# Attention values one step earlier, beside the next scores, in an encoder kernel

## The chip, the cores and the metric

The kernel runs on one core of a Trainium2 chip. The metric is the device time of one launch in microseconds. A core has a matrix engine (TensorE, PE in the profile, with its weight loads as PEld), a vector engine (VectorE, DVE), a scalar engine (ScalarE, ACT), GpSimd (POOL) and SyncE (SP), which here issues the transfers. Each engine works through its own queue in order, and semaphores make one wait for another.

## The reference, cut to what matters

The program is a trunk of two layers over 512 tokens of width 1024, in float32. Each layer normalizes x, makes one wide projection of it, computes two kinds of attention from parts of that projection, gates and mixes them, and ends with a gated feed-forward part (SwiGLU).

```python
z = h @ w_in
# a: differential attention, 4 heads, each with two softmaxes
s = einsum('bqhcd,bkhcd->bhcqk', qblk, kk) * scale
p = softmax(s, axis=-1)
a = p[:, :, 0] - lam_full * p[:, :, 1]
o = einsum('bhqk,bkhe->bqhe', a, v)          # then rms_norm of o
# b: three groups of window attention with dilation 1, 4 and 16, 8 heads each
s = where(mask, einsum('brnqhd,brnkhd->brnhqk', qb, kn) * scale, NEG_INF)
e = exp(s - max(s)); den = sum(e)
o = einsum('brnhqk,brnkhd->brnqhd', e, vn) / den
# the three groups are combined per head by a softmax over their log denominators
m = (sigmoid(g_A) * (a @ W_a) + sigmoid(g_B) * (b @ W_b)) @ W_out
```

## The kernel before

Float32 products are made from two halves. `split_part` cuts each weight tile into a rounded `whi` (a cast on ACT, L106 or L109) and a rest `wlo` (DVE, L107 or L110); the activations stand as `hTh` and `hTl`. `mm3` (lines 121 to 123) then issues three matmuls for each pair of tiles into a PSUM tile `pj`, of which there are three. All weights come through one stream of 1 MB transfers issued on SP (`load_raw`, L88), with two split weights held ready.

PE runs in the order in which the kernel's code issues its instructions (`manual_schedule`). The other engines' orders are laid out by a planner when the program is built: it goes by the order of issue as priority, by its own estimate of when each operand is ready, and lifts the weight splits ahead.

A layer projects in pieces. For each of two head pairs of the differential attention (`da_proj`) and for each of two times three window groups (`g_proj`) it makes q, k and v. A q or k piece is `ws_gen`: four steps of 12 matmuls of 512 columns ("wide"). A v piece (`proj_v`) is four steps of 24 matmuls of 256 columns ("narrow"). After q and k comes the rotary part `rope` on DVE (L415, L419) and GpSimd (L420, L421), which frees `pj`, and another split (L458, L459).

Attention is put between these steps. `drive` runs a projection and calls `att_step` after each of its steps; `att_step` advances the first job in `attq` by one step, and a job whose last scores are a period behind it lets the next one step as well. A job is a generator made by `pipeline`: each tile or batch i passes through stages, and stage f of tile i runs at step `period * i + lag`, with a period of 4. Stages that fall on the same step run in the order in which the tuple lists them.

- Differential attention (`da_attn`, four query tiles per head pair): `scores` (matmuls L484 with 32-row operands into the PSUM tiles `at0` to `at3`, the maxima L490, exponentials L492, and the difference of both softmaxes, L496 to L500), `turn` (PE transposes L510, copies L512), `values` (matmuls L519 into `at4`, then squares L525, a mean and a power on GpSimd L75, and L529, L530), and `finish` (transposes L537 into the other half of the same `at4`, and a split L540, L541).
- Window groups (`g_attn`; group 0 has two batches, groups 1 and 2 have one): `scores` (L583, then the mask L591, the maximum L593, exponentials L596), `turn` (transposes L610 and copies L611, or for group 2 a transpose on DVE, L606), and `values` (L628 for group 0, L631 for the others, in one or two parts, then copies L635 or L638).
- `combine` weighs the three groups of a head pair. It runs alone, once all jobs before it are done: small work on DVE and ACT, three steps later three PE transposes with multiplies (L687, L689) one step apart, then the sum and its split (L691 to L695).

`turn` has lag 3, `finish` 7, `scores` 0. The lags of `values` are in the lines that change. After the second head pair the gates are projected (`gate`, L736), and what is left of the queue is run out.

Of the kernel before, what the change touches and what calls it, by code (L numbers as in the profile page):

```python
# [23 lines left out]
NT = S // P  # L24
# [9 lines left out]
def encoder_trunk_kernel(  # L34
# [23 lines left out]
    def at(i, shape=(P, S)):  # L58
        return ps.tile(list(shape), F32, tag=f"at{i}", name=nm("at"), bufs=1)
# [4 lines left out]
    def small(n):  # L64
        return pp.tile([P, n], F32, tag=f"sm{n}", name=nm("sm"), bufs=8)
# [5 lines left out]
    def rstd_of(ss, n, scale, eps):  # L71
        t = small(n)
        nc.vector.tensor_scalar(out=t, in0=ss, scalar1=scale, scalar2=eps, op0=ALU.mult, op1=ALU.add)  # L73
        r = small(n)
        nc.gpsimd.tensor_tensor(out=r, in0=t, in1=mhalf[:, 0:n], op=ALU.pow)  # L75
        return r
# [310 lines left out]
    for l in range(depth):  # L387
# [17 lines left out]
        def et(shape=(P, S), dt=F32):  # L405
            return ip.tile(list(shape), dt, tag="e", name=nm("e"), bufs=8)
# [55 lines left out]
        def qk_scores(parts, qs, ks):  # L462
            n = len(parts)
            for j, (q, k) in enumerate(parts):
                for half in range(2):
                    for c in range(4):
                        r = slice(32 * c, 32 * c + 32)
                        yield c, q[r, half, qs], k[r, half, ks], j + half == 0, j + half == n
# [9 lines left out]
        def da_attn(u, qk, v):  # L478
            st = [dict() for _ in range(NT)]

            def scores(n):
                o = [at(c) for c in range(4)]
                for c, q, k, first, last in qk_scores(qk, slice(n * P, (n + 1) * P), slice(0, S)):
                    nc.tensor.matmul(o[c], q, k, start=first, stop=last)  # L484
                st[n].update(a=[], r=[])
                for h in range(2):
                    nmx, den, es = small(2), small(2), []
                    for c in range(2):
                        oc = o[2 * h + c]
                        nc.vector.tensor_reduce(out=nmx[:, c:c + 1], in_=oc, axis=AX.X, op=ALU.max, negate=True)  # L490
                        e = et()
                        nc.scalar.activation(out=e, in_=oc, func=AF.Exp, bias=nmx[:, c:c + 1],  # L492
                                             accum_out=den[:, c:c + 1])
                        es.append(e)
                    r = small(2)
                    nc.vector.reciprocal(out=r, in_=den)  # L496
                    nl = small(1)
                    nc.vector.scalar_tensor_tensor(out=nl, in0=den[:, 0:1], scalar=neglam, in1=r[:, 1:2],
                                                   op0=ALU.mult, op1=ALU.mult)
                    nc.vector.scalar_tensor_tensor(out=es[0], in0=es[1], scalar=nl, in1=es[0],  # L500
                                                   op0=ALU.mult, op1=ALU.add)
                    st[n]["a"].append(es[0])
                    st[n]["r"].append(r)

            def turn(n):
                st[n]["aT"] = []
                for h in range(2):
                    tp = at(h, (P, 4, P))
                    for kt in range(4):
                        nc.tensor.transpose(tp[:, kt, :], st[n]["a"][h][:, kt * P:(kt + 1) * P], ident)  # L510
                    aT = et((P, 4, P))
                    nc.scalar.copy(out=aT, in_=tp)  # L512
                    st[n]["aT"].append(aT)

            def values(n):
                oo = st[n]["o"] = at(4, (P, 4, P))
                for h in range(2):
                    for kt in range(4):
                        nc.tensor.matmul(oo[:, h, :], st[n]["aT"][h][:, kt, :], v[:, kt, h * P:(h + 1) * P],  # L519
                                         start=(kt == 0), stop=(kt == 3))  # L520
                on = et((P, 2, P))
                ss = small(2)
                rr = st[n]["r"]
                for g in range(2):
                    nc.scalar.activation(out=on[:, g, :], in_=oo[:, g, :], func=AF.Square, scale=rr[g][:, 0:1],  # L525
                                         accum_out=ss[:, g:g + 1])
                rs = rstd_of(ss, 2, 1.0 / P, SUBLN_EPS)
                for g in range(2):
                    nc.vector.tensor_tensor(out=rs[:, g:g + 1], in0=rs[:, g:g + 1], in1=rr[g][:, 0:1], op=ALU.mult)  # L529
                    nc.vector.scalar_tensor_tensor(out=on[:, g, :], in0=oo[:, g, :], scalar=rs[:, g:g + 1], in1=sg,  # L530
                                                   op0=ALU.mult, op1=ALU.mult)
                st[n]["on"] = on

            def finish(n):
                tp = st[n]["o"][:, 2:4, :]
                for g in range(2):
                    nc.tensor.transpose(tp[:, g, :], st[n]["on"][:, g, :], ident)  # L537
                qs = slice(n * P, (n + 1) * P)
                hv = oaT[0][:, 2 * u:2 * u + 2, qs]
                nc.scalar.copy(out=hv, in_=tp)  # L540
                nc.vector.tensor_tensor(out=oaT[1][:, 2 * u:2 * u + 2, qs], in0=tp, in1=hv.bitcast(F32),  # L541
                                        op=ALU.subtract)

            yield from pipeline(NT, 4, ((turn, 3), (finish, 7), (values, 5), (scores, 0)))

        def pipeline(n, period, stages):
            for j in range((n - 1) * period + max(lag for _, lag in stages) + 1):
                for f, lag in stages:
                    i, r = divmod(j - lag, period)
                    if r == 0 and 0 <= i < n:  # L550
                        f(i)
                yield j >= n * period
# [18 lines left out]
        def g_attn(gi, qk, v, vs, res):  # L571
            og, sts = g_out(gi)
            nb = 2 if gi == 0 else 4
# [40 lines left out]
            def values(b, part):  # L614
                o = at(4, (P, 2, 256))
                for i in range(2 * part, 2 * part + 2):
                    n = b * nb + i
                    cols = slice((n % 2) * P, (n % 2 + 1) * P)
                    for pr in range(2):
                        for kt in range(2 if gi == 0 else 1):  # L620
                            for hh in range(2):
                                h = 2 * pr + hh
                                hs = slice(h * DH, (h + 1) * DH)
                                pt = st[b]["pt"][h]
                                if gi == 0:
                                    s = WIN_START[n] + kt * P
                                    vt = v[:, s // P, hs] if s % P == 0 else vs[:, s // P, hs]
                                    nc.tensor.matmul(o[hh * DH:(hh + 1) * DH, pr, cols], vt, pt[:, 2 * i + kt, :],  # L628
                                                     start=(kt == 0), stop=(kt == 1))
                                else:  # L630
                                    nc.tensor.matmul(o[hh * DH:(hh + 1) * DH, pr, cols], v[:, n, hs], pt[:, i, :],  # L631
                                                     start=True, stop=True)
                if gi == 0:
                    for pr in range(2):
                        nc.scalar.copy(out=og[:, pr, :].rearrange("p (r s t) -> p t s r", r=4, s=4)[:, 16 * b:16 * b + 16],  # L635
                                       in_=o[:, pr, :].rearrange("p (t s r) -> p t s r", s=4, r=4))
                else:
                    nc.scalar.copy(out=og[:, :, 256 * part:256 * part + 256], in_=o)  # L638

            parts = [((lambda b, part=part: values(b, part)), 5 + part) for part in range(nb // 2)]  # L640
            yield from pipeline(NT // nb, 4, (*parts, (turn, 3), (scores, 0)))
            res.append((og, to_class(sts) if gi == 0 else sts))

# [79 lines left out]
        for u in range(2):  # L723
            res = []
            for gi in range(3):
                att_push(g_attn(gi, *drive(g_proj(gi)), res), DELAY[1 + gi])
            att_push(combine(u, res), 0, True)
# [153 lines left out]
```

## Time and profile before

| what | value |
|---|---|
| median of 3 runs | 1857.94 us (1857.57 to 1859.06) |
| profiled execution | 1857.75 us, of which the span from first to last instruction is 1856.0 us |
| mean granted TensorE clock | 0.996 |
| PE busy | 1819.6 us, 98% of the span |
| DVE, ACT, POOL busy | 917.7, 668.2, 159.1 us |
| longest waits of PE in all | 12.5 us for the first normalized tiles (L244 for L238), 5.9 and 2.4 us for the split of h (L122 for L247, L121 for L246) |

A line of the groups or the timeline names the source line, the engine, the operation, the tile written and the tiles read, the active rows and columns of a matmul, the shape and the count. PE's durations overlap, since matmuls are pipelined: what a matmul costs is read from one start to the next. In the timeline the number in brackets is the idle time before the row and what ended it. Layer one takes the first half of the span, layer two the second, with the same waits.

### The profile page before, as it was taken

Reading aid. Unit: us, or ns where it says so; the run is one execution under the profiler, and the core shown is the slowest. Engines: PE = TensorE matmul, PEld = TensorE weight load, DVE = VectorE, ACT = ScalarE, POOL = GpSimd, SP = SyncE. Lnnn points to the kernel's source line nnn. Section 1 sums busy time; section 2 is a strip of 40 time slices with the busy share of each in tenths; the row PEclk is TensorE's granted clock in tenths of the full one; section 3 lists DMA queues with packets and bytes.
Section 4 is the critical chain, followed back from the end, with each engine's and each line's share of the span. In section 5 each row is a group of like instructions: output and inputs, shape, how many; then the busy total and the mean of one; then the engine's idle time right before and its main releaser. Section 6 shows DMA issues by size and latency. Waiting matters only on the chain. (4 is left out here: it accounts for less than half of the span.)

```text
span 1856.0 us, 25587 instructions
## 1 busy us (share of the span) xinstructions
PE 1819.6 (98%) x10784; PEld 1542.3 (83%) x10784; DVE 917.7 (49%) x1255; ACT 668.2 (36%) x1301; POOL 159.1 (9%) x128
## 2 busy tenths in 40 slices
PE   6999999999999999999999999999999999999997
PEld 6888897888889888888888888888888788888886
DVE  5667758545355333322456776675445543333222
ACT  3444453353234223222234444443523332322221
POOL 1212011101000000000011121111011000000000
PEclk9999999999999999999999999999999999999999
DMA  6322123222444322232432322322234423322332
GB/s 186 104 68 87 60 75 102 67 86 91 133 138 151 112 91 91 94 110 91 147 118 78 96 65 69 111 63 87 71 108 148 149 94 105 99 91 91 107 109 68
DMA packets 145186, 186.26 MB, mean 100 GB/s; under 512 B 7216, under 2 KB 130480, under 8 KB 145072
## 3 DMA queue, kind: packets, MB, share of 16 engines
q1 hardware_dynamic: 145072, 184.63, 31.2%
q8 instruction: 84, 1.38, 0.3%
q14 instruction: 30, 0.25, 0.0%
HBM read 174.06 MB, written 10.55 MB: 99 GB/s over the span
## 5 line engine op out<-in xcount | busy, mean ns | idle before, releaser
L121 PE MATMUL pj<-hTh,whi 128*128 128x512 f32 (+1 forms) x1536 | 588.9, 383 | 2.4 <-ACT hTh L246 2.4
L122 PE MATMUL pj<-hTl,whi 128*128 128x512 f32 (+1 forms) x1536 | 581.2, 378 | 5.9 <-DVE hTl L247 5.9
L123 PE MATMUL pj<-hTh,wlo 128*128 128x512 f32 (+1 forms) x1536 | 580.0, 378 | 0.0
L107 DVE TENSOR_TENSOR wlo<-raw,whi 128x1024 fp32r<-128x1024 f32 x252 | 331.4, 1315 | 456.2 <-ACT whi L106 455.9
L106 ACT CAST whi<-raw 128x1024 fp32r<-128x1024 f32 x252 | 264.6, 1050 | 733.6 <-PE pj L122 490.8
L121 PEld LDWEIGHTS pj<-hTh,whi 128*128 128x128 f32 x1536 | 291.4, 190 | 63.2 <-issue 6.8
L122 PEld LDWEIGHTS pj<-hTl,whi 128*128 128x128 f32 x1536 | 291.5, 190 | 56.8 <-DVE hTl L247 7.4
L123 PEld LDWEIGHTS pj<-hTh,wlo 128*128 128x128 f32 x1536 | 291.3, 190 | 53.5
L121 PE MATMUL pj<-whi,hTh 128*128 128x256 f32 x512 | 147.5, 288 | 0.0
L122 PE MATMUL pj<-wlo,hTh 128*128 128x256 f32 x512 | 144.8, 283 | 0.0
L123 PE MATMUL pj<-whi,hTl 128*128 128x256 f32 x512 | 144.8, 283 | 0.0
L75 POOL TENSOR_TENSOR sm<-sm,mhalf 128x1 f32<-128x1 f32 (+1 forms) x48 | 33.2, 692 | 921.8 <-DVE sm L73 921.8
L596 ACT ACTIVATE e<-e,gst 128x128 f32<-128x128 f32 (+1 forms) x192 | 81.4, 426 | 81.6 <-DVE gst L593 81.4
L121 PEld LDWEIGHTS pj<-whi,hTh 128*128 128x128 f32 x512 | 98.0, 191 | 3.2 <-issue 2.8
L122 PEld LDWEIGHTS pj<-wlo,hTh 128*128 128x128 f32 x512 | 98.1, 192 | 0.2
L123 PEld LDWEIGHTS pj<-whi,hTl 128*128 128x128 f32 x512 | 98.0, 191 | 0.0
L806 DVE TENSOR_TENSOR s<-s,pj 128x512 f32<-128x512 f32 x42 | 28.9, 688 | 123.6 <-PE pj L123 123.6
L285 PE MATMUL at<-whi,ac 128*128 128x512 f32 x200 | 78.8, 394 | 0.0
L284 PE MATMUL at<-whi,ac 128*128 128x512 f32 x200 | 78.5, 392 | 0.0
L286 PE MATMUL at<-wlo,ac 128*128 128x512 f32 x200 | 77.7, 388 | 0.0
L492 ACT ACTIVATE e<-at,sm 128x512 f32<-128x512 f32 x64 | 43.8, 686 | 76.4 <-DVE sm L490 76.4
L591 DVE TENSOR_TENSOR e<-at,mk 128x512 f32<-128x512 f32 x64 | 41.2, 682 | 40.1 <-PE at L583 40.1
(175 smaller groups left out, 2347.4 us busy)
## 6 DMA issues: line engine op xcount, KB each, us to landing
raw<-in_w_in_dram SPq DMA_DIRECT2D x64, 1024.0 KB, 5.7
raw<-in_w_gate_up_dram SPq DMA_DIRECT2D x44, 1024.0 KB, 5.0
raw<-in_w_down_dram SPq DMA_DIRECT2D x22, 1024.0 KB, 4.9
raw<-in_w_out_dram SPq DMA_DIRECT2D x8, 1024.0 KB, 4.9
xs<-m SPq DMA_DIRECT2D x12, 512.0 KB, 2.9
m<-xs SPq DMA_DIRECT2D x12, 512.0 KB, 4.9
m<-in_x_dram SPq DMA_DIRECT2D x32, 128.0 KB, 5.2
raw<-in_w_a_dram SPq DMA_DIRECT2D x8, 512.0 KB, 3.4
```

Of the source, the lines that this page charges most:

```text
L75: nc.gpsimd.tensor_tensor(out=r, in0=t, in1=mhalf[:, 0:n], op=ALU.pow)
L106: nc.scalar.copy(out=shp(hi), in_=src)
L107: nc.vector.tensor_tensor(out=shp(lo), in0=src, in1=shp(hi.bitcast(F32)), op=ALU.subtract)
L121: nc.tensor.matmul(o, ah, bh, start=(i == 0), stop=False)
L122: nc.tensor.matmul(o, ah, bl, start=False, stop=False)
L123: nc.tensor.matmul(o, al, bh, start=False, stop=(i == n - 1))
L284: nc.tensor.matmul(o, ah, hi[:, sl], start=(k == 0), stop=False)
L285: nc.tensor.matmul(o, al, hi[:, sl], start=False, stop=False)
L286: nc.tensor.matmul(o, ah, lo[:, sl], start=False, stop=(k == nk - 1))
L492: nc.scalar.activation(out=e, in_=oc, func=AF.Exp, bias=nmx[:, c:c + 1], accum_out=den[:, c:c + 1])
L591: nc.vector.tensor_tensor(out=e, in0=o[h], in1=mask, op=ALU.add)
L596: nc.scalar.activation(out=e[:, i, :], in_=e[:, i, :], func=AF.Exp, bias=sts[:, n, h:h + 1], accum_out=sts[:, n, 4 + h:5 + h])
```

## The change

The lag of `values` goes from 5 to 4 in both kinds of attention (from 5 and 6 to 4 and 5 where there are two parts). With a period of 4 the values of a tile or batch then fall on the step of the next one's scores, and stand ahead of them, since the tuple lists `values` before `scores`. No instruction is added or taken away.

```diff
             def da_attn(u, qk, v):
...
-            yield from pipeline(NT, 4, ((turn, 3), (finish, 7), (values, 5), (scores, 0)))
+            yield from pipeline(NT, 4, ((turn, 3), (finish, 7), (values, 4), (scores, 0)))
...
             def g_attn(gi, qk, v, vs, res):
...
-            parts = [((lambda b, part=part: values(b, part)), 5 + part) for part in range(nb // 2)]
+            parts = [((lambda b, part=part: values(b, part)), 4 + part) for part in range(nb // 2)]
             yield from pipeline(NT // nb, 4, (*parts, (turn, 3), (scores, 0)))
```

## The prediction

> **What bounds the kernel now.** I read the page first (share of each engine), then the waits of TensorE (PE), then PE's timeline around the attention steps, then that of VectorE (DVE) where PE waited.
>
> ```profile
> span 1856.0 us, 25587 instructions
> PE 1819.6 (98%) x10784; PEld 1542.3 (83%) x10784; DVE 917.7 (49%) x1255; ACT 668.2 (36%) x1301; POOL 159.1 (9%) x128
> ```
>
> PE is busy for 98% of the span, and its order is written by hand, so a change of order can win or lose two things only: what PE loses where it passes from one kind of matmul to another, and where it stands still for another engine. The first is seen in the starts of PE's instructions (start, duration, engine, line); two rows of the groups by line, with the mean in ns behind the comma, give durations used below.
>
> ```profile
> 65.11 0.39 PE L123 MATMUL pj<-hTh,wlo 128*128 128x512 f32 x1
> 65.43 1.67 PE L484 MATMUL at<-op,op 32*128 32x512 f32 x24
> 67.02 0.50 PE L121 MATMUL pj<-hTh,whi 128*128 128x512 f32 x1
> 67.36 0.39 PE L122 MATMUL pj<-hTl,whi 128*128 128x512 f32 x1
> 67.59 0.39 PE L123 MATMUL pj<-hTh,wlo 128*128 128x512 f32 x1
> ...
> 83.82 0.39 PE L123 MATMUL pj<-hTh,wlo 128*128 128x512 f32 x1
> 84.05 1.95 PE L519 MATMUL at<-m,e 128*128 128x128 f32 x16
> 85.75 0.36 PE L121 MATMUL pj<-whi,hTh 128*128 128x256 f32 x1
> 85.95 0.28 PE L122 MATMUL pj<-wlo,hTh 128*128 128x256 f32 x1
> 86.07 0.29 PE L123 MATMUL pj<-whi,hTl 128*128 128x256 f32 x1
> ```
>
> A wide projection matmul starts 0.23 us after the one before it (67.36 to 67.59), so a step of 12 is 2.72 us; a narrow one starts after 0.12, so a step of 24 is 2.88 us. Scores of the differential attention (L484, 32-row operands) cost two surcharges: they start 0.32 after the last projection (0.09 more than 0.23), and the second projection behind them comes 0.34 after the first (0.11 more). The values (L519, 128x128 operands) start at the usual 0.23; the row's 1.95 less the 0.275 that one lasts, over 15, is 0.11 a matmul, so 16 are 1.79, and the block with the longer first gap behind it is 1.70 + 0.08. An interruption by these values costs nothing.
>
> ```profile
> L519 PE MATMUL at<-m,e 128*128 128x128 f32 x256 | 31.1, 275 | 0.0
> ...
> L530 DVE SCALAR_TENSOR_TENSOR e<-at,sm,sg 128x128 f32<-128x128 f32 x32 | 9.8, 347 | 0.0
> ```
>
> ```profile
> 249.03 1.09 PE L631 MATMUL at<-e,m 128*64 128x128 f32 x16
> 250.05 2.07 PE L583 MATMUL at<-op,op 32*128 32x128 f32 x64
> 252.05 0.50 PE L121 MATMUL pj<-hTh,whi 128*128 128x512 f32 x1
> ```
>
> This is the one place where a window group's values (128x64 operands) and the next scores stand together already, at the second half of group 1.
>
> **The change, part by part.** Counting the steps of the queue with lag 5 and with lag 4 gives, for each of the two layers, 55 places where attention stands between projections before, and 45 after. Eleven blocks of values move in front of the scores that followed one step behind: eight of the differential attention (the last tile of each head pair joins the next job's first scores), three of group 0. One joint place is lost: group 1's second half now comes a step before group 2's first scores. Groups 1 and 2 and the combine that waits for them run one step earlier. No instruction is added or removed.
>
> *Passages.* Differential values cost nothing where they stood, so joining them to scores wins nothing if values-to-scores costs the 0.09 of projection-to-scores. No row shows that pair. If it is hidden like projection-to-values, 8 x 0.09 = 0.7 us a layer is won; if it is as dear as L631-to-L583 (16 matmuls take 1.02, so 0.2 from the last start, about 0.15 over its pace), 8 x 0.06 = 0.5 is lost. I take 0, since both full-height matmuls shown above hand over to each other freely. [...] A joint of group values and scores saves one 0.09 and one 0.11: 0.2, with two more joints a layer: **-0.4**.
>
> *The turns behind the joined scores.* Scores go through reduce, exponential and L500 before the transposes of `turn`, three steps later. Until now the values' 1.70 + 0.08 us lay in between. That cover is gone.
>
> ```profile
> 74.41 1.74 DVE L500 SCALAR_TENSOR_TENSOR e<-e,sm,e 128x512 f32<-128x512 f32 x1
> ...
> 88.56 1.75 DVE L500 SCALAR_TENSOR_TENSOR e<-e,sm,e 128x512 f32<-128x512 f32 x1
> ...
> 152.50 1.75 DVE L500 SCALAR_TENSOR_TENSOR e<-e,sm,e 128x512 f32<-128x512 f32 x1
> ...
> 183.86 1.27 DVE L500 SCALAR_TENSOR_TENSOR e<-e,sm,e 128x512 f32<-128x512 f32 x1
> ```
>
> ```profile
> 76.29 0.63 PE L510 MATMUL at<-ident,e 128*128 128x128 f32 x4 [0.39 <-DVE e L500]
> ...
> 91.59 0.82 PE L510 MATMUL at<-ident,e 128*128 128x128 f32 x6
> ...
> 154.86 1.04 PE L510 MATMUL at<-ident,e 128*128 128x128 f32 x8
> ...
> 186.47 1.03 PE L510 MATMUL at<-ident,e 128*128 128x128 f32 x8
> 187.65 0.44 PE L537 MATMUL at<-ident,e 128*128 128x128 f32 x2
> ```
>
> The very first turn has no values before it and waits already: L500 ends at 76.15, and PE goes on at 76.29, 0.14 later. The second head's four transposes come 0.44 after the turn starts. So the first of the seven later tiles has 91.59 + 0.44 - 90.31 = 1.72 us to spare, the worst 154.86 + 0.44 - 154.25 = 1.05, the last 186.47 + 0.44 - 185.13 = 1.78. In the same two views two others have 1.31 and 1.38, and the last two, on narrow steps, over 2.7. Less 1.78, plus 0.14, these are late by 0.20, 0.87, 0.14, 0.61 and 0.54: **+2.4** a layer. If the small norm instructions of the values, now ahead of the scores, leave DVE's chain, it could be 1.2; if they push into it (about 0.7 each, two L530 of 0.35), 5.
>
> What waits behind: next to the late turn stands `finish`. The last turn above was held up by it (186.47 to 187.65 is 1.18, not 0.88), since the normed values came late; they now have a step and the scores more time: **-0.3**. The values of tile n+1 follow one step after `finish` of tile n, whose tile `at4` they overwrite; ACT and DVE must have read it. I take 0, and up to 0.6 in one place a layer. Values that stand where scores stood need the same copies that those scores waited for (L512, L611): 0. SP's small transfers of group 0's statistics are issued one step earlier, ahead of a weight load; two weights are held ready, so 0. POOL's power step of the norm moves ahead of the ropes on its queue; POOL is busy 9% of the span, so 0.
>
> *Values one step earlier with no scores beside them.* For group 2 the turn is a DVE transpose. PE rows, then DVE rows:
>
> ```profile
> 266.22 0.55 PE L631 MATMUL at<-e,m 128*64 128x128 f32 x6
> ...
> 395.67 0.44 PE L631 MATMUL at<-e,m 128*64 128x128 f32 x4
> ```
>
> ```profile
> 263.71 0.69 DVE L606 STREAM_TRANSPOSE e<-e 128x512 f32<-128x512 f32 x1
> ...
> 392.87 0.71 DVE L606 STREAM_TRANSPOSE e<-e 128x512 f32<-128x512 f32 x1
> ```
>
> The fourth transpose ends at 264.40, and the fifth matmul of the moved values would need it at 266.22 - 2.88 + 0.25 = 263.59; in the second pair of heads 393.58 against 395.67 - 2.72 + 0.25 = 393.20. With the 0.14: 0.95 + 0.52 = **+1.5** (0.5 to 2).
>
> *The combine one step earlier.* Here DVE is behind, and PE pays:
>
> ```profile
> 296.96 1.71 PE L583 MATMUL at<-op,op 32*128 32x256 f32 x48
> ...
> 306.90 2.16 PE L610 MATMUL at<-ident,e 128*128 128x128 f32 x12
> 309.31 0.93 PE L610 MATMUL at<-ident,e 128*128 128x128 f32 x4 [0.26 <-ACT e L596]
> ...
> 312.94 0.38 PE L583 MATMUL at<-op,op 32*128 32x256 f32 x1
> ...
> 314.83 1.69 PE L583 MATMUL at<-op,op 32*128 32x256 f32 x45 [0.22 <-DVE e L611]
> ```
>
> ```profile
> 285.75 1.07 DVE L415 TENSOR_TENSOR r<-pj,cos 128x512 f32<-128x512 f32 x1 [2.44 <-PE pj L123]
> ...
> 302.64 1.28 DVE L591 TENSOR_TENSOR e<-at,mk 128x512 f32<-128x512 f32 x2
> ```
>
> 16 transposes at 0.11 last 1.8; these end at 310.24, 3.34 after their start: 1.5 lost. The scores lose 1.9 between 312.94 and 314.83. The cause is that the masks (L591) of the second head pair's group 0 start at 302.64 though their scores (296.96) were done some 4 us before: the combine's multiplies and split stand ahead of them in DVE's queue. One step earlier, the combine's first multiplies fall into the 2.44 us in which DVE was idle. Masks 2.4 to 3.2 us earlier free the turn wholly, and of the 1.9 leave about 0.5: **-2.9** (0 to -3.4).
>
> Sum a layer: 0 - 0.4 + 2.4 - 0.3 + 1.5 - 2.9 = +0.3; two layers +0.6. The profiled execution took 1857.75 us (span 1856.0 and 1.75 around it), 0.2 under the median of 1857.94. So **1858.3**.
>
> **The rivals.** *A, the forecast: gains and losses cancel*, 0.2% or 3.7 us being about what a measurement of this kernel can tell from no change. For it: every term is of 0.3 to 3 us, and they have both signs.
>
> *B, slower: the late turns.* The joined scores leave DVE too little time, and the combine's relief does not come, because DVE merely fills the gap with the same queue in another order. With turns at 2.4, the group values at 1.5, passages and `finish` at -0.7 and relief at -0.5, a layer is +2.7, the kernel 1863.2. It decides once a layer's terms together pass +1.9, which with the full group values needs relief under 1.3. Against it: DVE has idle time right where the combine moves.
>
> *C, faster: the relief without the late turns.* If the values' norm leaves the chain of the scores, the turns cost 1.2, the group values 1.0 and relief is -3.4: -1.9 a layer with the rest, 1853.9.
>
> *D, the clock.* Differential values and scores together are 1.70 + 1.59 = 3.3 us without a projection. If the granted clock fell over such a stretch, 22 following steps of 2.7 us at half pace would cost some 60 us: 1917. Against it, the stretch that exists:
>
> ```profile
> 249.03:252.05 3.02, 3.02 (x82) 2.73 (x81) 0.00 (x0) 0.58 (x1) 0.00 (x0) 1.00 0.96 299
> ```
>
> PE is busy in all of it and its clock is 1.00 (third column from the right). One in a hundred is left for the 0.3 us by which the new blocks are longer. [...]
>
> **How the numbers follow.** A 0.60, B 0.22, C 0.17, D 0.01. The time is A's, 1858.3, with its own range 1854.2 to 1861.6 (within 3.7 of the median). Of B and C I keep the nearer part: 1853.5 reaches just past C's sum, 1863.8 just past B's; turns at 5 a layer with the full relief (1863.5) lie inside, and so does each end of the passages and of the values put alone to the forecast's sum. Chances: faster 0.17, same 0.60, slower 0.23.
>
> **What the profile after would show.** Right: L519 directly before L484, with a start of L484 about 0.2 after the last L519; PE waits on L510 for L500 in several turns of a layer, 0.1 to 0.9 us each, where one is seen now; values of group 2 waiting for L606; L591 of the second pair's group 0 some 3 us earlier against its scores, and the turn at L610 back to 1.9. It would be wrong if DVE or ACT got another order: their queues are laid out by a planner, and a rope or weight split put ahead of a reduce moves each of these waits by about 1 us.

## The result: slower by 0.6%, and the profile after

| | before | after |
|---|---|---|
| median of 6 runs each | 1859.18 us (1857.57 to 1863.02) | 1870.20 us (1869.13 to 1871.62) |
| ratio | | 1.0058, 95% interval 1.0045 to 1.0071 |
| span of the profiled execution | 1856.0 us | 1868.4 us |
| first L484 to the layer's next normalization (L244), layers one and two | 487.17, 487.18 us | 493.52, 493.61 us |

The forecast was 1858.3 with a range up to 1863.8, so it was wrong, and on the slower side. The last row of the table says where: both layers lose the same 6.4 us, all of it in the stretch in which attention stands between the projections. The page of the kernel after:

```profile
span 1868.4 us, 25595 instructions
PE 1819.5 (97%) x10784; PEld 1544.0 (83%) x10784; DVE 916.4 (49%) x1255; ACT 671.6 (36%) x1301; POOL 155.4 (8%) x128
PEclk9999999999999999999999999999999999999999
```

PE is busy for the same 1819 us as before and its mean granted clock is the same 0.996; the 12.4 us are time in which it stands still. The waits of PE name what for (total us, times, longest):

```profile
PE at L510 <- DVE e L500: 14.9, 12, 1.7
...
PE at L631 <- DVE e L606: 1.0, 2, 0.5
PE at L628 <- DVE e L611: 0.7, 4, 0.2
...
PE at L519 <- DVE big L541: 0.3, 2, 0.2
```

The first line stood at 0.8 us in two places before. It is the transposes of `turn` waiting for the difference of the two softmaxes. The other three are small: group 2's values behind L606, group 0's behind the copies L611, and the values behind `finish`'s split (L541), whose tile `at4` they overwrite. The turn of the second tile and the worst turn, in PE's timeline:

```profile
79.53 1.95 PE L519 MATMUL at<-m,e 128*128 128x128 f32 x16
81.41 1.67 PE L484 MATMUL at<-op,op 32*128 32x512 f32 x24
83.01 0.50 PE L121 MATMUL pj<-hTh,whi 128*128 128x512 f32 x1
...
91.60 0.60 PE L510 MATMUL at<-ident,e 128*128 128x128 f32 x4
93.27 0.63 PE L510 MATMUL at<-ident,e 128*128 128x128 f32 x4 [1.07 <-DVE e L500]
...
158.07 0.60 PE L510 MATMUL at<-ident,e 128*128 128x128 f32 x4
160.36 0.63 PE L510 MATMUL at<-ident,e 128*128 128x128 f32 x4 [1.69 <-DVE e L500]
...
164.13 2.05 PE L519 MATMUL at<-m,e 128*128 128x128 f32 x16 [0.15 <-DVE big L541]
```

The values stand directly before the next scores, as forecast. The second head's four transposes should follow 0.44 after the first four; they follow 1.67 and 2.29 after, so these turns are late by 1.23 and 1.85. DVE around the first of them, after and then before, tells the reason:

```profile
82.36 0.17 DVE L73 TENSOR_SCALAR sm<-sm 128x2 f32<-128x2 f32 x1 [2.08 <-ACT e L525]
83.35 0.23 DVE L529 TENSOR_TENSOR sm<-sm,sm 128x1 f32<-128x1 f32 x2 [0.82 <-POOL sm L75]
83.54 0.61 DVE L530 SCALAR_TENSOR_TENSOR e<-at,sm,sg 128x128 f32<-128x128 f32 x2
84.07 1.28 DVE L490 TENSOR_REDUCE sm<-at 128x1 f32<-128x512 f32 x2
...
91.40 1.73 DVE L500 SCALAR_TENSOR_TENSOR e<-e,sm,e 128x512 f32<-128x512 f32 x1
```

```profile
81.28 1.29 DVE L490 TENSOR_REDUCE sm<-at 128x1 f32<-128x512 f32 x2 [1.02 <-PE at L484]
...
88.45 0.15 DVE L73 TENSOR_SCALAR sm<-sm 128x2 f32<-128x2 f32 x1
88.56 1.75 DVE L500 SCALAR_TENSOR_TENSOR e<-e,sm,e 128x512 f32<-128x512 f32 x1
90.91 0.23 DVE L529 TENSOR_TENSOR sm<-sm,sm 128x1 f32<-128x1 f32 x2 [0.60 <-POOL sm L75]
91.10 0.61 DVE L530 SCALAR_TENSOR_TENSOR e<-at,sm,sg 128x128 f32<-128x128 f32 x2
```

Before, the reduces (L490) start as soon as the scores release them, and the norm of the values (L73, a step on GpSimd, L529, L530) runs behind, partly after L500. After, the norm was issued ahead of the scores and stands ahead of their reduces in DVE's queue. The last of the scores ends at 83.08 (81.41 and 1.67); the reduces start at 84.07, since DVE waits for GpSimd's power until 83.35 and then needs 0.72 for L529 and L530. Of its wait of 0.82 only the last 0.27 lie behind the end of the scores.

Adding up, for the first layer, the time from the start of each block on PE to the start of what follows it gives the whole loss by line:

| PE time by block, us a layer | before | after | difference |
|---|---|---|---|
| projections | 401.97 | 400.08 | -1.9 |
| turn and finish (L510, L537) | 9.05 | 16.85 | +7.8 |
| values (L519, L628, L631) | 29.39 | 33.74 | +4.35 |
| scores of the groups (L583) | 16.97 | 14.50 | -2.5 |
| group turns (L610) | 11.84 | 10.41 | -1.4 |
| L484, L687 | 17.94 | 17.94 | 0 |

The row of the values grows for three reasons: the hand-over of L519 to the scores now counts there and no longer with the projections (1.6, with 0.2 of waits for `at4`), L628 waits for the copies that the scores waited for before (1.4, against the -2.5 of the scores), and L631 of group 2 waits for L606 (1.4).

### The profile page after: what moved, and what is told of

It is laid out like the page before. It is cut to its first block, busy times and chain, and to the rows that moved or that the text cites. A ratio compares the mean times of both kernels' runs of the same rounds, so it can differ in the third digit from the quotient of the medians.

```text
span 1868.4 us, 25595 instructions
## 1 busy us (share of the span) xinstructions
PE 1819.5 (97%) x10784; PEld 1544.0 (83%) x10784; DVE 916.4 (49%) x1255; ACT 671.6 (36%) x1301; POOL 155.4 (8%) x128
## 5 line engine op out<-in xcount | busy, mean ns | idle before, releaser
L122 PE MATMUL pj<-hTl,whi 128*128 128x512 f32 (+1 forms) x1536 | 580.9, 378 | 5.9 <-DVE hTl L247 5.9
L122 PEld LDWEIGHTS pj<-hTl,whi 128*128 128x128 f32 x1536 | 291.4, 190 | 57.4 <-DVE hTl L247 7.4
L122 PE MATMUL pj<-wlo,hTh 128*128 128x256 f32 x512 | 144.8, 283 | 0.0
L75 POOL TENSOR_TENSOR sm<-sm,mhalf 128x1 f32<-128x1 f32 (+1 forms) x48 | 28.8, 599 | 984.5 <-DVE sm L73 984.5
L122 PEld LDWEIGHTS pj<-wlo,hTh 128*128 128x128 f32 x512 | 98.1, 192 | 0.5
```

What stands on the lines that cost most here:

```text
L122: nc.tensor.matmul(o, ah, bl, start=False, stop=False)
```

## Experiments

Attention stages are given as the time from the first L484 to L244 in layer one; before it is 487.17, after 493.52. Lateness of a turn is the start of the second head's transposes less that of the first head's, less 0.44. Each ratio is to the kernel before, run beside the changed one (medians 1858.8 to 1860.3).

**The two halves of the change.**

```diff
-            yield from pipeline(NT, 4, ((turn, 3), (finish, 7), (values, 5), (scores, 0)))
+            yield from pipeline(NT, 4, ((turn, 3), (finish, 7), (values, 4), (scores, 0)))
```

> Only the differential attention's lag goes to 4; the window groups keep 5. If the loss sits in that half (turns at L510 late, 7.0 us a layer in the trace after against 0.3 and the first turn's 0.6 before): 14 us over the kernel before, ratio 1.0075. If the loss were a joint effect of both edits or sat in the groups' moved values: within 4 us of the kernel before.

Measured: 1876.33 us, ratio 1.0091 (1.0078 to 1.0104). The stage takes 496.02 us, 8.9 more than before. In layer two it takes 497.70: there eight matmuls from 1248.64 on start 0.43 apart instead of 0.23, at a granted clock of 0.50 (1249 to 1251), which adds 1.7. Layer one has the same edit and no such stretch.

```diff
-            parts = [((lambda b, part=part: values(b, part)), 5 + part) for part in range(nb // 2)]
+            parts = [((lambda b, part=part: values(b, part)), 4 + part) for part in range(nb // 2)]
```

> Only the window groups' lags go to 4 and 5. From the two traces, a layer: group 2's values wait for L606, +1.4; the turn and values of the second pair's group 0, -2.7; group joints -0.4; the rest +0.2: -1.5, so 3 us faster than before, ratio 0.9984. If the relief came from the differential attention's edit instead: 2 to 3 us slower.

Measured: 1851.86 us, ratio 0.9959 (0.9947 to 0.9970); the stage takes 484.68, 2.5 less. In layer one the halves add up: 8.9 - 2.5 = 6.4, and in layer two within 0.2 once the 1.7 of the clock are taken off. The differential half is the loss, the groups' half a gain.

**The norm behind the scores.** The norm of `values` becomes a stage of its own, listed behind `scores`, on the same step (its lines move down by 3: `finish` is L540, the norm's last lines L532 and L533).

```diff
+            def norm(n):
+                oo = st[n]["o"]
...
-            yield from pipeline(NT, 4, ((turn, 3), (finish, 7), (values, 4), (scores, 0)))
+            yield from pipeline(NT, 4, ((turn, 3), (finish, 7), (values, 4), (scores, 0), (norm, 4)))
```

> The changed kernel, with the values' norm (L525, L73, L75, L529, L530) cut off into a stage of its own that is issued on the same step behind the scores; PE's order is that of the changed kernel. Theory 1 (DVE's order: the norm stands ahead of the reduces L490, which start 1.06 us after the scores instead of 0.10): reduces start 0.1 after the scores again, late turns fall from 7.0 to about 2.4 us a layer, 1861, ratio to before 1.001. Theory 2 (PE's cover alone: 1.8 us of values no longer stand between scores and turn): nothing changes, 1870, ratio 1.006.

Measured: 1871.55 us, ratio 1.0070 (1.0057 to 1.0082): nothing won. The time is near the one that theory 2 named, but not for its reason, since the turns did change. Waits of PE, then PE and DVE at the turn that was the worst:

```profile
PE at L540 <- DVE e L533: 9.1, 11, 1.7
...
PE at L510 <- DVE e L500: 3.4, 7, 0.7
```

```profile
158.18 0.60 PE L510 MATMUL at<-ident,e 128*128 128x128 f32 x4
159.51 0.63 PE L510 MATMUL at<-ident,e 128*128 128x128 f32 x4 [0.73 <-DVE e L500]
160.82 0.44 PE L540 MATMUL at<-ident,e 128*128 128x128 f32 x2 [0.68 <-DVE e L533]
```

```profile
149.97 1.29 DVE L490 TENSOR_REDUCE sm<-at 128x1 f32<-128x512 f32 x2 [3.78 <-PE at L484]
...
157.61 1.75 DVE L500 SCALAR_TENSOR_TENSOR e<-e,sm,e 128x512 f32<-128x512 f32 x1
159.96 0.23 DVE L532 TENSOR_TENSOR sm<-sm,sm 128x1 f32<-128x1 f32 x2 [0.59 <-POOL sm L75]
160.16 0.61 DVE L533 SCALAR_TENSOR_TENSOR e<-at,sm,sg 128x128 f32<-128x128 f32 x2
```

The reduces start with the scores again, and the turns are late by 0.23, 0, 0.53, 0, 0.90, 0.61 and 0.17 behind the first: the sizes that the prediction had worked out. But now the norm comes last, and `finish` beside the turn waits for it by 0.3 to 1.9 in six places, 5.6 us a layer. The theory that the order of the two on DVE was all that was wrong has fallen. The wait moved from the transposes of `turn` to those of `finish`.

**The norm left out.** Both kernels once without the norm: the values are only copied, so its squares, its power and its multiplies are missing from the work.

```diff
-                ss = small(2)
...
-                    nc.vector.scalar_tensor_tensor(out=on[:, g, :], in0=oo[:, g, :], scalar=rs[:, g:g + 1], in1=sg,
-                                                   op0=ALU.mult, op1=ALU.mult)
+                nc.scalar.copy(out=on, in_=oo[:, 0:2, :])
```

> The changed kernel with the norm of the differential values left out (L525, L73, L75, L529, L530; a plain copy on ACT hands the values to finish). Theory 3 (the way from scores to turn and finish has lost 1.8 us of PE work, and DVE's queue on that way, reduces, differences, norm, ropes and weight rests, no longer fits, whichever of norm and difference comes last): with the norm gone the turns are late by what the prediction had, about 2.4 us a layer instead of 8, and the time is 1859 to 1861. If the loss has nothing to do with DVE's queue (passages, at4): still 1868 or more.

> The kernel before with the same norm left out: the baseline for the run above. The values still stand between scores and turn, so no turn but the first of a layer waits and the wait of finish (0.4 us a layer) goes: 1858, ratio 0.9995. Theory 3: the two runs without norm differ by 4 us at most, where the two with norm differ by 11.

Measured: from the kernel after, 1857.78 us, ratio 0.9995 (0.9985 to 1.0004), stage 487.59; from the kernel before, 1858.31, ratio 0.9993 (0.9983 to 1.0004), stage 486.74. So the norm costs 0.4 us a layer where it stood and 5.9 where it was moved. The same turn of the changed kernel without it, in PE's timeline:

```profile
155.74 0.60 PE L510 MATMUL at<-ident,e 128*128 128x128 f32 x4
157.08 0.63 PE L510 MATMUL at<-ident,e 128*128 128x128 f32 x4 [0.74 <-DVE e L500]
```

It is late by 0.90 instead of 1.85. All turns of a layer together are late by 3.4 us (0.55 of it the first, as before), against 8.5 with the norm. So the missing 1.78 us of PE cover cost 2.8 us a layer by themselves, and the norm in DVE's way another 5.2 (8.54 - 3.38). Without the norm in either kernel the change costs 0.85 a layer (487.59 - 486.74).

**Scores ahead of the values.** The new lags, but with `scores` listed first, so that PE's values are cover for DVE again.

```diff
-            yield from pipeline(NT, 4, ((turn, 3), (finish, 7), (values, 5), (scores, 0)))
+            yield from pipeline(NT, 4, ((turn, 3), (finish, 7), (scores, 0), (values, 4)))
...
-            parts = [((lambda b, part=part: values(b, part)), 5 + part) for part in range(nb // 2)]
-            yield from pipeline(NT // nb, 4, (*parts, (turn, 3), (scores, 0)))
+            parts = [((lambda b, part=part: values(b, part)), 4 + part) for part in range(nb // 2)]
+            yield from pipeline(NT // nb, 4, ((scores, 0), *parts, (turn, 3)))
```

> The changed lags, with scores listed ahead of values in both pipelines: attention interrupts in as few places, but the values stand behind the scores again and cover the way to the turn. Both theory 1 and theory 2: no late turns beyond the first one of a layer, and the groups' gain stays: 1855 to 1857, ratio 0.998. If the loss came from joining as such (passages of PE, or the shared tile at4 one step after finish): 1865 or more.

Measured: 1859.04 us, ratio 0.9998 (0.9990 to 1.0007), stage 488.17, some 2 us above what was expected. Waits of PE, then a group's scores:

```profile
PE at L537 <- DVE e L530: 1.7, 2, 0.9
PE at L583 <- DVE e L611: 1.3, 6, 0.2
...
PE at L510 <- DVE e L500: 0.8, 2, 0.4
```

```profile
210.46 0.38 PE L583 MATMUL at<-op,op 32*128 32x256 f32 x2
211.06 0.38 PE L583 MATMUL at<-op,op 32*128 32x256 f32 x1 [0.22 <-DVE e L611]
211.66 1.69 PE L583 MATMUL at<-op,op 32*128 32x256 f32 x45 [0.22 <-DVE e L611]
```

The wait for L500 is back at 0.8, and no turn but the first of a layer is late, so the same joint in the other order gives the cover back. It wins nothing all the same: scores that stand directly behind a turn lose 1.1 us twice a layer to the copies L611 (three matmuls take the 1.2 from 210.46 to 211.66, where the 45 behind them take 1.69), so the groups' gain at the scores is gone (L583 16.8 a layer, before 17.0, after 14.5). A `finish` waits for the norm again (1.7 in two places), the values take 2.5 a layer more than before (group 2's wait for L606 is 1.4 of it), and the shorter projections save only 1.1.

**Which part of the groups' half wins.** With the lag of group 2 kept, the combine runs no step earlier:

```diff
-            parts = [((lambda b, part=part: values(b, part)), 5 + part) for part in range(nb // 2)]
+            parts = [((lambda b, part=part: values(b, part)), (5 if gi == 2 else 4) + part) for part in range(nb // 2)]
```

> Only groups 0 and 1 at the new lag; group 2 and so the combine stay where they were. If the combine's step made the relief: the waits of group 2's values for L606 (1.37 us a layer) are gone, but the second pair's group 0 is late again by about 2.5 us a layer, and the time is 1857 to 1858, ratio 0.999. If group 0's own move made it: 1849, below the run with all groups moved.

and with the lags of before, only the combine's own delay is cut by a step:

```diff
-            for _ in range(3):
+            for _ in range(2):
                 yield True
```

> The kernel before, all lags at 5, with the combine's transposes two steps behind its weights instead of three: the one step earlier that the change brought it. If the relief (turn L610 and scores L583 of the second pair's group 0, 3.3 us a layer late before) comes from that alone: L591 starts 2 to 3 us earlier against its scores, 2.6 us a layer, 1853.8, ratio 0.997, and no waits for L606. If it came from the moved values of group 0: no change.

Measured: the first 1855.12 us, ratio 0.9975 (0.9965 to 0.9985), stage 485.88, between its two expectations; the second 1852.82, ratio 0.9961 (0.9948 to 0.9973), stage 484.96. PE of the first, then PE and DVE of the second, at the second head pair's group 0:

```profile
307.34 2.17 PE L610 MATMUL at<-ident,e 128*128 128x128 f32 x12
309.77 0.93 PE L610 MATMUL at<-ident,e 128*128 128x128 f32 x4 [0.26 <-ACT e L596]
```

```profile
298.37 1.69 PE L583 MATMUL at<-op,op 32*128 32x256 f32 x48
308.28 1.91 PE L610 MATMUL at<-ident,e 128*128 128x128 f32 x16
```

```profile
301.77 1.28 DVE L591 TENSOR_TENSOR e<-at,mk 128x512 f32<-128x512 f32 x2
```

With the combine a step earlier the masks start 3.40 after the start of their scores (5.68 before, by the prediction's rows), and the turn is whole, 1.91. With the values moved and the combine not, the turn is broken up as before: the relief of the turn, 1.4, comes from the combine alone. Of the wait behind it for the copies L611 the earlier combine takes 0.8 (L583 at this place lasts 2.72 instead of 3.52), which makes 2.2 in all; the moved values of group 0 take another 0.4 there, for the values (3.35) and scores (1.63) together last 4.98 where before it was 3.52 and 1.90. The first kernel has no wait for L606 either, since group 2 stayed where it was.

**Both, without the costs.** Groups 0 and 1 moved, group 2 and the differential pairs kept, the combine's delay cut by one step, as shown, then by two (`range(1)`):

```diff
-            parts = [((lambda b, part=part: values(b, part)), 5 + part) for part in range(nb // 2)]
+            parts = [((lambda b, part=part: values(b, part)), (5 if gi == 2 else 4) + part) for part in range(nb // 2)]
...
-            for _ in range(3):
+            for _ in range(2):
```

> What the runs point to: differential values and group 2 stay where they were (lag 5), groups 0 and 1 move (lag 4), and the combine's transposes come one step earlier by themselves. Both gains together, a layer: passages -0.4 to -0.8, the second pair's turn -1.4, its values or scores -1.2 to -1.8, the first pair's -0.4, no waits for L606: -3.5, 1851 to 1852, ratio 0.996 or a little below. Rival: the two gains are the same DVE time counted twice, and it stays at the 0.9961 of the combine alone.

> The same with the combine's transposes two steps earlier than in the kernel before. If DVE's queue is what delays the second pair's group 0, its last wait for L611 (about 0.7 us a layer with one step) shrinks further: up to 1 us faster than the run above. If one step has already taken the combine out of its way: no difference; and if the weights that ACT spreads (L679) are not ready so soon, the first L687 waits and it is slower.

Measured: with one step 1849.15 us, ratio to before 0.9945 (0.9933 to 0.9958); with two 1851.21, ratio 0.9951 (0.9937 to 0.9965). The first has the lowest time of all kernels here, though the intervals of these two overlap. Its stage takes 483.6, 3.6 less than before, about the sum of its two parts (2.2 and 1.3). Two layers make 7.2, but the span is 9.5 shorter. Its page and the same place:

```profile
span 1846.5 us, 25589 instructions
PE 1812.6 (98%) x10784; PEld 1539.7 (83%) x10784; DVE 918.0 (50%) x1255; ACT 669.1 (36%) x1301; POOL 159.0 (9%) x128
```

```profile
296.44 1.69 PE L583 MATMUL at<-op,op 32*128 32x256 f32 x48
306.35 1.91 PE L610 MATMUL at<-ident,e 128*128 128x128 f32 x16
```

The other 2.3 lie outside the attention stage, and the clock alone makes up more than that. Here is PE behind a wait of 1.88 for the split of h (L122 for L247) that both kernels have in layer two, before and then with the joined edits:

```profile
1480.20 0.41 PE L122 MATMUL pj<-hTl,whi 128*128 128x256 f32 x1
1480.41 0.41 PE L123 MATMUL pj<-hTh,wlo 128*128 128x256 f32 x1
```

```profile
1471.39 0.28 PE L121 MATMUL pj<-hTh,whi 128*128 128x256 f32 x1
1471.51 0.28 PE L122 MATMUL pj<-hTl,whi 128*128 128x256 f32 x1
```

These matmuls start 0.21 apart before and 0.12 apart now. From 1479.4 to 1482.8 the granted clock before is 0.50, and again from 933.3 to 936.7. Each stretch costs about 1.5 us: from the end of the wait to the next transposes (L244) PE needs 7.23 and 7.30 us for 47 matmuls, which at 0.12 would take some 5.7. In the execution with the joined edits neither occurs, and its mean granted clock is 0.998 (before 0.996). So the attention stage is the better measure of an edit here than the whole time: the runs with the groups alone, the early combine and this one lie 7.2, 6.0 and 11.2 us below the kernel before, of which their two stages account for 5.0, 4.5 and 7.2.

With two steps the combine's last wait goes too, but the scores and group 0's values at the same place take 0.3 and 0.4 longer (2.02 instead of 1.69 for the L583 block at 296.20), and the stage is 0.3 longer.

## Why the prediction was wrong

Its terms for a layer, against the blocks of the table and the waits in them:

| term | predicted | measured |
|---|---|---|
| passages (measured: what the other rows leave) | -0.4 | -0.8 |
| turns behind the joined scores, and `finish` | +2.4 - 0.3 | +7.8 |
| values waiting for `at4` | 0, up to 0.6 | +0.5 |
| group 2's values waiting for L606 | +1.5 | +1.4 |
| combine one step earlier (second pair's group 0) | -2.9 | -2.7, of it -2.2 by the combine alone |
| first pair's group 0 | not counted | +0.2 |
| sum | +0.3 | +6.4 |

**The step that failed** is "The turns behind the joined scores". Its mechanism was right: the values' 1.78 us had been DVE's cover, and without them the turns are late. The middle value of 2.4 holds for exactly that: it is 2.8 with the norm left out and 2.4 with the norm behind the scores. The miss is the norm. The prediction saw that its instructions now stand ahead of the scores, gave this 0 in the forecast and let the turns come to 5 at most. Measured are 7.9 for the blocks of L510, and 5.2 of the lateness go when the norm is left out. The prediction's own price, "about 0.7 each", was right: L529 and L530 hold the reduces up by 0.72 (83.35 to 84.07). What was wrong is that the middle value left it out, and that the upper bound was too low by its own terms, since 0.7 on each of the five late turns over 2.4 is 5.9 and not 5. On top comes something that it had no term for: behind the end of the scores DVE stands still for another 0.27 to 0.34 (in layer one), because its queue holds L529 for GpSimd's power, and with it the reduces behind, whose data are there. A lateness of 1.06 at the reduces instead of 0.10, counted from the start of the projection behind the scores, reaches the turn undiminished wherever there is no slack (in the worst turn 1.85 against 0.90).

**The gain for `finish`** came (no wait after; the normed values are ready 7 to 10 us ahead), but the same order on DVE paid for it. With the norm behind the scores the turns are as forecast and `finish` pays 5.6. DVE's work between the scores and the step of these transposes no longer fits into that time without the PE work that was moved: of the two orders tried, each lets one of the two transposes wait, and with the norm left out 0.85 of the loss is left.

**Rival B** named this mechanism, "the late turns", but with the wrong price and a condition that was not needed: it let the relief fail. The relief came nearly in full, and turns at 7.8 carried the kernel past B's 1863.2 all the same. The range ended where turns at 5 ended. **Rival C** had the norm leave the chain; it did the opposite. **Rival D** did not happen in this kernel: taken 4 us at a time, the granted clock does not fall below 0.97 anywhere in its two attention stages. The PEclk row of the page could not have shown it, for one of its digits covers 47 us. Its price was wrong too, for no run shows 22 steps at half pace: where the clock does fall inside an attention stage, as in layer two with the differential half alone, it costs 1.7 us, and the two falls in the kernel before, outside these stages, last 3.4 us and cost some 1.5 each. That a stretch without a projection lowers the clock was not shown.

**What held.** In eight joints the values lose 0.09 a joint at their hand-over to the scores, as much as projections lose, so those joints are worth 0: the middle value. The late values of group 2 came with their sign and size. The relief came with its sign and a little smaller (masks at 3.40 behind their scores' start, after too, so 2.3 earlier and not 2.4 to 3.2). The prediction took both from single rows of DVE. The chances of faster, same and slower were tied to these terms and gave slower 0.23.

L500 itself is part of the tightness. It lasts 1.73 to 1.75 in the rows above where GpSimd works on the rotary part, for instance here in the kernel after, on GpSimd and then on DVE:

```profile
156.38 2.05 POOL L421 TENSOR_TENSOR r<-r,r 128x512 f32<-128x512 f32 x1 [6.26 <-DVE r L415]
158.41 1.26 POOL L420 TENSOR_TENSOR r<-r,r 128x512 f32<-128x512 f32 x1
```

```profile
154.53 0.75 DVE L500 SCALAR_TENSOR_TENSOR e<-e,sm,e 128x512 f32<-128x512 f32 x1
...
158.49 1.73 DVE L500 SCALAR_TENSOR_TENSOR e<-e,sm,e 128x512 f32<-128x512 f32 x1
```

The first head's L500 takes 0.75 with GpSimd idle, the second head's 1.73 beside L420, and ends 0.55 after it. It is so in both kernels: of the 64 L500 in the two traces the 40 with GpSimd idle take 0.74 to 0.75, the 20 beside L420 alone or with L75 take 1.72 to 1.76, and the four that run beside L421 1.26 to 1.32. Why they take longer was not shown. That the 1.0 us would come off the late turns if the rotary part stood elsewhere was not tried.

## What to carry to other kernels

PE work between a producer and the step that consumes its result is cover for the other engines: before moving it, subtract it from the slack of every later consumer, and do so for the engine's whole queue: what is issued ahead of the chain counts with its full duration, and with the pauses in which it waits for a third engine. When a wait disappears after a reorder, look whose result now comes last. A change made of two equal edits in two places should be costed, and tried, by halves: here one half loses 0.9% and the other wins 0.4%. Where single executions differ by stretches of lower clock, compare the stage that the edit touches.

## What the runs showed of the hardware

- The first 32-row matmul starts 0.20 to 0.21 after the last start of the block before it, both behind 128x128 matmuls (L519, pace 0.11, as at 81.41 after) and behind 128x64 ones (L628 and L631, pace 0.06, as at 218.51 after and 250.05 before).
- PE's busy time says nothing of such a change: PE was busy 1819.6 and 1819.5 us in kernels 12.4 us apart.
- A power on two columns on GpSimd (L75) holds DVE's queue for 0.6 to 0.8 us (0.59, 0.60 and 0.82 in the rows above), about as long as the two multiplies behind it take (0.61 for both L530).
- The granted clock fell to 0.50 for 3.4 us at a time, in some executions and not in others: behind the wait of L122 for L247 twice in the profiled execution of the kernel before (933.3 to 936.7 and 1479.4 to 1482.8) and twice after (939.6 to 943.0 and 1492.6 to 1496.0), not behind the same wait in that of the joined version, where the mean is 0.998. The 50 executions of the kernel before that were run beside the experiments follow their mean granted clock: 1861.6 us on average at 0.994 (3 of them), 1858.4 at 0.996 (18), 1856.5 at 0.998 (5).
